# The last three pieces' products for the second tokens in two column halves, and the output in pieces of 1024 columns

## The chip, the cores and the metric

The kernel runs on one core of a Trainium2 chip. The metric is the device time of one execution in microseconds. A core has a matrix engine (TensorE; PE in the profile, with PEld for its weight loads), a vector engine (VectorE, DVE), an activation engine (ScalarE, ACT), GpSimd (POOL) and SyncE (SP), whose queue issues nearly all transfers here. Each engine works through its own queue in order; engines wait for each other through semaphores. Products are accumulated in PSUM, in banks of 512 fp32 columns on 128 partitions; everything else lies in SBUF.

## The reference

One layer of a gated short-convolution decoder, with 256 tokens of 2048 features, everything in fp32, and a normalization behind it:

```python
h = rmsnorm(x, norm_g[layer])
h, gate = adaln(h, c, ada_w[layer], ada_b[layer])
y = short_conv_mixer(h, sc_w_in[j], sc_conv_w[j], sc_w_out[j])
x = x + gate[:, None, :] * y
return rmsnorm(x, final_g)
```

`adaln` makes shift, scale and gate from a conditioning vector. The mixer projects 2048 features to four branches of 4096, convolves along the tokens over three taps, multiplies the branches together and projects 4096 back to 2048: `jnp.einsum('bse,ed->bsd', y, w_out)`. The last line needs, for every token, the mean of the squares of all 2048 features before any feature can be written.

## The kernel before

Weights and activations are each split into a high and a low part (`split` makes `hi` on ScalarE and `lo` on VectorE), and every product is the sum of three: high by high, high by low, low by high. The layer starts with the normalization and the conditioning, then come the input projection in pieces (line 430, tiles `mm_s` and `mm_b`, 256 tokens wide), the convolution and the gates, whose results `ys` stay in SBUF. Those parts are the same in both kernels.

The output projection runs over four column groups `dc` of 512 features. For each, the weights come in eight pieces (`ep`, four blocks of 128 rows each, 1 MB), and `out_mm` multiplies a piece by the tokens: 4 blocks x 3 products, each 128 tokens by 512 columns. The tokens are in two tiles of 128, the first (`t = 0`) and the second (`t = 1`). `po[0]` and `po[1]` are the accumulators of the two, each a PSUM bank of 512 columns.

The last group, `dc = 3`, differs. The gate is multiplied into the weights (line 668), and the banks are filled with the residual beforehand (line 656, ScalarE), so that what stands in a bank at the end is the new feature itself. `po[0]` and `po[1]` are in two different tiles of PSUM. For the last three pieces (`LATE = 3`) the second tokens' products are put off in the source: they stand behind the first tokens' end. So the first tokens are finished early: `gated(0, ...)` squares the bank on ScalarE and sums the squares into a column of `fsq` (line 685); `finish(0)` takes the root of that sum plus `part_sum`, the sum over the other three groups (line 633, which needs a change of ScalarE's table), its reciprocal on VectorE (line 634), multiplies the four column groups of the token tile by it (lines 639 to 643) and stores them (line 644). Then the 36 late products of the second tokens, `gated(1, ...)` and `finish(1)`.

The order in each queue isn't the source's alone. A scheduler with a cost model sets it when the program is built: some of the late products are pulled forward to places between the first tokens' products. The same layer puts in the semaphore waits: an instruction waits for those that wrote what it reads, and for those that read or wrote what it overwrites.

Of the kernel before, what the change touches and what calls it, by code (L numbers as in the profile page):

```python
# [10 lines left out]
AF = mybir.ActivationFunctionType  # L11
ALU = mybir.AluOpType

P = 128
D = 2048
# [113 lines left out]
def short_conv_layer(ctx: ExitStack, tc: tile.TileContext, x, c, norm_g, ada_w, ada_b, w_in, conv_w, w_out, final_g, out):  # L129
    nc = tc.nc  # L130
# [138 lines left out]
    for t in range(TT):  # L269
        for dh in range(2):  # L270
# [3 lines left out]
            else:  # L274
                nc.vector.scalar_tensor_tensor(
                    out=junk[:, t], in0=xt[t][dh], scalar=1.0, in1=xt[t][dh], op0=ALU.mult, op1=ALU.mult,
# [32 lines left out]
    scale = const.tile([P, KT], F32, tag="scale", name="scale")  # L309
# [21 lines left out]
    def split(raw, n, lo_tag="lo"):  # L331

        hi = wpool.tile([P, SLOT], F32R, tag="hi", name="hi", bufs=3)
        lo = wpool.tile([P, SLOT], F32R, tag=lo_tag, name="lo", bufs=3)
        nc.scalar.copy(hi[:, :n], raw[:, :n])  # L335
        nc.vector.tensor_tensor(out=lo[:, :n], in0=raw[:, :n], in1=hi[:, :n].bitcast(F32), op=ALU.subtract)  # L336
        return hi, lo
# [197 lines left out]
    def gate(dc):  # L535
        return gates[dc // 2][:, dc % 2, :]
# [31 lines left out]
    for ct in range(NS, NCT, 2):  # L568
        for q in QUARTERS:
            bank = psum.tile([P, CT, T], F32, tag="mm", name="mm_b")[:, 0:2]  # L570
            col = q * E + ct * P
            for kp in range(0, KT, KP):
# [5 lines left out]
                hi, lo = split(raw, SLOT)  # L578
                for m in range(2):
                    for i in range(KP):  # L580
                        k = kp + i
                        o = slice((i * 2 + m) * P, (i * 2 + m + 1) * P)
# [24 lines left out]
    big = hpool.tile([P, 4, D], F32, tag="big", name="big")  # L607
    fg = big[:, 2, :]
# [3 lines left out]
    fsq = const.tile([P, TT, 4], F32, tag="fsq", name="fsq")  # L612
    EP = 4
    LATE = 3

    def out_mm(po, t, ep, hi, lo):
        for i in range(EP):
            ct = ep * EP + i
            y = ys[ct // 2][:, ct % 2]
            yh = y[:, 0, t * P : (t + 1) * P]  # L620
            yl = y[:, 1, t * P : (t + 1) * P]
            o = slice(i * 512, (i + 1) * 512)
            opens = ct == 0 and dc < 3
            nc.tensor.matmul(po, yh, hi[:, o], start=opens, stop=False, skip_group_check=True)  # L624
            nc.tensor.matmul(po, yh, lo[:, o], start=False, stop=False, skip_group_check=True)  # L625
            nc.tensor.matmul(po, yl, hi[:, o], start=False, stop=ct == NCT - 1, skip_group_check=True)  # L626

    part_sum = const.tile([P, TT], F32, tag="part_sum", name="part_sum")

    def finish(t):  # L630

        fs = const.tile([P, 1], F32, tag="fs", name="fs", bufs=2)
        nc.scalar.activation(fs, fsq[:, t, 3:4], AF.Sqrt, bias=part_sum[:, t : t + 1])
        nc.vector.reciprocal(fs, fs)
        for c0, n, vector in ((0, 512, True), (512, 512, False), (1536, 512, True), (1024, 512, False)):
            dd = slice(c0, c0 + n)
            r = big[:, t, dd]
            if c0 == 1536:
                nc.vector.scalar_tensor_tensor(out=r, in0=po[t], scalar=fs, in1=fg[:, dd], op0=ALU.mult, op1=ALU.mult)
            elif vector:  # L640
                nc.vector.tensor_scalar_mul(r, r, fs)
            else:
                nc.scalar.activation(r, r, AF.Copy, scale=fs)  # L643
            nc.sync.dma_start(out[t * P : (t + 1) * P, dd], r)

    for dc in range(4):
        dcs = slice(dc * 512, (dc + 1) * 512)

        both = [psum.tile([P, TT, 512], F32, tag="mm", name="mm_o") for _ in range(1 + (dc == 3))]
        po = [both[-t][:, t] for t in range(TT)]  # L650
        n_ep = NCT // EP
        late = []
        if dc == 3:

            for t in range(TT):
                nc.scalar.copy(po[t], big[:, t, dcs])
        for ep in range(n_ep):

            first = dc == 0 and ep == 0
            raw = wpool.tile([P, SLOT], F32, tag="raw" if first else "lo", name="raw_o", bufs=3)  # L660
            nc.sync.dma_start(
                raw.rearrange("p (k f) -> p k f", k=EP),
                w_out[0, ep * EP * P : (ep + 1) * EP * P, dcs].rearrange("(k p) f -> p k f", p=P),
            )
            if dc == 3:

                raw3 = raw.rearrange("p (k f) -> p k f", k=EP)
                nc.vector.tensor_tensor(
                    out=raw3, in0=raw3, in1=gate(dc).unsqueeze(1).to_broadcast([P, EP, 512]), op=ALU.mult
                )  # L670
            hi, lo = split(raw, SLOT, "raw")
            out_mm(po[0], 0, ep, hi, lo)
            if dc == 3 and ep >= n_ep - LATE:
                late.append((ep, hi, lo))
            else:
                out_mm(po[1], 1, ep, hi, lo)

        def gated(t, bank, c0, n):

            cs = slice(dc * 512 + c0, dc * 512 + c0 + n)  # L680
            r = big[:, t, cs]
            p0 = (dc % 2) * 1024 + t * 512 + c0
            pr = big[:, 3, p0 : p0 + n]
            if dc == 3:
                nc.scalar.activation(pr, bank, AF.Square, scale=D**-0.5, accum_out=fsq[:, t, dc : dc + 1])
                return
            nc.vector.tensor_tensor(out=pr, in0=bank, in1=gate(dc)[:, c0 : c0 + n], op=ALU.mult)
            nc.vector.tensor_tensor(out=r, in0=r, in1=pr, op=ALU.add)
            nc.scalar.activation(pr, r, AF.Square, scale=D**-0.5, accum_out=fsq[:, t, dc : dc + 1])
            nc.vector.tensor_tensor(out=r, in0=r, in1=fg[:, cs], op=ALU.mult)  # L690
            if dc == 2:
                ps = part_sum[:, t : t + 1]
                nc.vector.reduce_sum(ps, fsq[:, t, 0:3], axis=mybir.AxisListType.X)
                nc.vector.tensor_scalar_add(ps, ps, EPS)

        gated(0, po[0], 0, 512)
        if dc == 3:
            finish(0)
        for ep, hi, lo in late:
            out_mm(po[1], 1, ep, hi, lo)  # L700
        gated(1, po[1], 0, 512)
    finish(1)


# [22 lines left out]
```

## Time and profile before

| what | us |
|---|---|
| median of 3 runs | 922.97 (922.72 to 924.28) |
| the profiled execution | 922.73 |
| its span, from first to last instruction | 921.0 |
| TensorE busy in it | 905.1 |
| granted TensorE clock, mean | 0.994 of full |

A profile row names the line of the code, the engine, the operation and the tiles. "Releaser" is what ended a wait. Starts are counted from the start of the span. The ends of products are modelled: in a dense row the time between two starts is the pace, and it is shorter than the duration shown. In the output stage all 768 products have the same shape, 128 tokens by 512 columns.

### The profile page before, as it was taken

What the parts mean: (1) busy time and instruction counts of PE and PEld (TensorE: products, weight loads), DVE (VectorE), ACT (ScalarE), POOL (GpSimd) and SP (SyncE); (2) the same over time, 40 slices, a digit from 0 to 9 for tenths busy, and PEclk for the clock granted to TensorE, in tenths of its full rate; (3) what the DMA queues carried; (4) which work ended last, traced back from release to release, by engine and by line L of the source; (5) the groups of instructions that cost most, each with busy time, mean ns of one, the idle gap of its engine ahead of it and who ended that gap; (6) DMA issues with size and microseconds to landing.
All of it is one profiled execution on the core that took longest, in us unless ns stands there. A gap on an engine that the chain in (4) does not pass through costs nothing.

```text
span 921.0 us, 16348 instructions
## 1 busy us (share of the span) xinstructions
PE 905.1 (98%) x7119; PEld 871.3 (95%) x7119; DVE 627.0 (68%) x601; ACT 450.3 (49%) x427; POOL 0.7 (0%) x6
## 2 busy tenths in 40 slices
PE   7899999999999999999999999999999999999996
PEld 7899999999999999999999999999999988888885
DVE  5888898999875899986545544555454535555882
ACT  3778975545544755544443334433444333443333
POOL 0000000000000000000000000000000000000000
PEclk9899999999999999999999999999999999999999
DMA  9999999999995569867566656665666486565542
GB/s 313 368 382 357 344 336 360 342 348 344 353 347 200 184 214 353 276 209 229 186 200 200 192 185 194 203 198 184 191 188 201 142 330 229 192 205 195 184 137 91
DMA packets 147367, 227.64 MB, mean 247 GB/s; under 512 B 5424, under 2 KB 103904, under 8 KB 146912
## 3 DMA queue, kind: packets, MB, share of 16 engines
q1 hardware_dynamic: 147056, 226.51, 73.2%
q8 instruction: 55, 0.90, 0.4%
q10 hardware_dynamic: 240, 0.09, 0.0%
q14 instruction: 16, 0.13, 0.0%
HBM read 224.49 MB, written 2.10 MB: 246 GB/s over the span
## 4 chain that ended last, share of the span: by engine, by line
PE 95%; DMA 3%; SPq 1%; DVE 0%; ACT 0%; ACTq 0%; issue 0%; DVEq 0%
PE mm_b L430 38%; PE mm_s L430 37%; PE mm_o L625 6%; PE mm_o L626 6%; PE mm_o L624 6%; DMA at<-in_ada_w_dram 2%; DMA x<-in_x_dram 1%; DMA raw_s<-in_sc_w_in_dram 1%; PE ps_gate L563 0%; SPq L223 0%; PE tp_g L419 0%; PE tp_x L305 0%; DVE lo L336 0%; SPq L203 0%; SPq L399 0%; ACT big L643 0%
## 5 line engine op out<-in xcount | busy, mean ns | idle before, releaser
L430 PE MATMUL mm_s<-hT,hi 128*128 128x256 f32 x2048 | 353.0, 278 | 1.0 <-ACT hT L325 0.5
L430 PE MATMUL mm_b<-hT,hi 128*128 128x256 f32 x2048 | 348.8, 276 | 0.0
L430 PEld LDWEIGHTS mm_s<-hT,hi 128*128 128x128 f32 x2048 | 310.6, 189 | 2.1 <-ACT hT L325 0.7
L430 PEld LDWEIGHTS mm_b<-hT,hi 128*128 128x128 f32 x2048 | 308.3, 188 | 0.2 <-issue 0.2
L430 PE MATMUL mm_s<-hT,lo 128*128 128x256 f32 x1024 | 283.1, 278 | 1.8 <-DVE lo L336 1.8
L430 PE MATMUL mm_b<-hT,lo 128*128 128x256 f32 x1024 | 282.6, 276 | 0.0
L336 DVE TENSOR_TENSOR lo<-raw,hi 128x2048 fp32r<-128x2048 f32 (+1 forms) x66 | 148.0, 2243 | 128.1 <-ACT hi L335 128.1
L335 ACT CAST hi<-raw 128x2048 fp32r<-128x2048 f32 (+1 forms) x66 | 123.7, 1874 | 203.8 <-PE mm_b L430 149.9
L430 PEld LDWEIGHTS mm_s<-hT,lo 128*128 128x128 f32 x1024 | 192.9, 189 | 2.0 <-DVE lo L336 2.0
L430 PEld LDWEIGHTS mm_b<-hT,lo 128*128 128x128 f32 x1024 | 192.2, 188 | 0.2 <-issue 0.2
L335 ACT CAST hi<-raw_s 128x2048 fp32r<-128x2048 f32 (+1 forms) x64 | 121.6, 1901 | 102.6 <-PE mm_s L430 88.9
L336 DVE TENSOR_TENSOR lo<-raw_s,hi 128x2048 fp32r<-128x2048 f32 (+1 forms) x64 | 145.4, 2273 | 33.2 <-ACT hi L335 30.3
L336 DVE TENSOR_TENSOR lo<-raw_o,hi 128x2048 fp32r<-128x2048 f32 x32 | 73.3, 2291 | 66.1 <-ACT hi L335 66.1
L335 ACT CAST hi<-raw_o 128x2048 fp32r<-128x2048 f32 x32 | 61.0, 1907 | 106.9 <-PE mm_o L626 88.0
L625 PE MATMUL mm_o<-lo,y 128*128 128x512 f32 x256 | 99.7, 391 | 0.0
L624 PE MATMUL mm_o<-hi,y 128*128 128x512 f32 x256 | 99.3, 389 | 0.0
L626 PE MATMUL mm_o<-hi,y 128*128 128x512 f32 x256 | 99.3, 389 | 0.0
L412 DVE SCALAR_TENSOR_TENSOR gv<-at,silu_c,gv 128x512 f32<-128x512 f32 x105 | 78.5, 749 | 2.5 <-DMA at<-in_ada_w_dram 0.8
L625 PEld LDWEIGHTS mm_o<-lo,y 128*128 128x128 f32 x256 | 48.1, 188 | 10.1 <-issue 0.2
L626 PEld LDWEIGHTS mm_o<-hi,y 128*128 128x128 f32 x256 | 48.0, 188 | 10.1 <-issue 0.2
L624 PEld LDWEIGHTS mm_o<-hi,y 128*128 128x128 f32 x256 | 48.1, 188 | 10.0
L451 ACT COPY acc<-mm_s 128x1024 f32<-128x1024 f32 x43 | 43.5, 1014 | 18.1 <-PE mm_s L430 18.0
(94 smaller groups left out, 382.2 us busy)
## 6 DMA issues: line engine op xcount, KB each, us to landing
raw<-in_sc_w_in_dram SPq DMA_DIRECT2D x64, 1024.0 KB, 5.6
raw_s<-in_sc_w_in_dram SPq DMA_DIRECT2D x63, 1024.0 KB, 7.0
raw_o<-in_sc_w_out_dram SPq DMA_DIRECT2D x32, 1024.0 KB, 5.2
at<-in_ada_w_dram SPq DMA_DIRECT2D x114, 256.0 KB, 6.8
at_g<-in_ada_w_dram SPq DMA_DIRECT2D x32, 512.0 KB, 7.0
at<-in_ada_w_dram SPq DMA_DIRECT2D x6, 512.0 KB, 8.8
x<-in_x_dram SPq DMA_DIRECT2D x4, 512.0 KB, 6.1
big<-in_x_dram SPq DMA_DIRECT2D x2, 1024.0 KB, 9.6
```

The lines of the kernel that those rows point to most:

```text
L335: nc.scalar.copy(hi[:, :n], raw[:, :n])
L336: nc.vector.tensor_tensor(out=lo[:, :n], in0=raw[:, :n], in1=hi[:, :n].bitcast(F32), op=ALU.subtract)
L412: nc.vector.scalar_tensor_tensor(out=gv, in0=at4[:, i], scalar=c_k, in1=gv, op0=ALU.mult, op1=ALU.add)
L430: mm = last_mm[0] = nc.tensor.matmul(dst, w, h[:, k], start=begins and left, stop=ends, skip_group_check=True)
L451: nc.scalar.copy(acc[ch, q], bank)
L624: nc.tensor.matmul(po, yh, hi[:, o], start=opens, stop=False, skip_group_check=True)
L625: nc.tensor.matmul(po, yh, lo[:, o], start=False, stop=False, skip_group_check=True)
L626: nc.tensor.matmul(po, yl, hi[:, o], start=False, stop=ct == NCT - 1, skip_group_check=True)
```

## The change

Two things change, both at the end of `dc = 3`.

The late products of the second tokens run over columns 0 to 255 of the bank first, all 36 of them, and then over columns 256 to 511, another 36; both halves are in the same PSUM bank. Each half is squared by itself. Both squares sum into the same column of `fsq`; VectorE adds the first one's sum to `part_sum` between the two.

`finish` works in two pieces of 1024 columns for both token tiles: ScalarE multiplies columns 512 to 1023 and VectorE 0 to 511, and one store of 512 KB writes both; then ScalarE takes 1024 to 1535, VectorE 1536 to 2047, and a second store writes these. Before, there were four stores of 256 KB.

```diff
-    def out_mm(po, t, ep, hi, lo):
+    def out_mm(po, t, ep, hi, lo, c0=0, n=512):
+        po = po[:, c0 : c0 + n]
...
-            o = slice(i * 512, (i + 1) * 512)
+            o = slice(i * 512 + c0, i * 512 + c0 + n)
...
-        for c0, n, vector in ((0, 512, True), (512, 512, False), (1536, 512, True), (1024, 512, False)):
-            dd = slice(c0, c0 + n)
-            r = big[:, t, dd]
-            if c0 == 1536:
-                nc.vector.scalar_tensor_tensor(out=r, in0=po[t], scalar=fs, in1=fg[:, dd], op0=ALU.mult, op1=ALU.mult)
-            elif vector:
-                nc.vector.tensor_scalar_mul(r, r, fs)
-            else:
-                nc.scalar.activation(r, r, AF.Copy, scale=fs)
-            nc.sync.dma_start(out[t * P : (t + 1) * P, dd], r)
+        r = big[:, t]
+        nc.scalar.activation(r[:, 512:1024], r[:, 512:1024], AF.Copy, scale=fs)
+        nc.vector.tensor_scalar_mul(r[:, 0:512], r[:, 0:512], fs)
+        nc.sync.dma_start(out[t * P : (t + 1) * P, 0:1024], r[:, 0:1024])
+        nc.scalar.activation(r[:, 1024:1536], r[:, 1024:1536], AF.Copy, scale=fs)
+        nc.vector.scalar_tensor_tensor(
+            out=r[:, 1536:D], in0=po[t], scalar=fs, in1=fg[:, 1536:D], op0=ALU.mult, op1=ALU.mult
+        )
+        nc.sync.dma_start(out[t * P : (t + 1) * P, 1024:D], r[:, 1024:D])
...
                 nc.scalar.activation(pr, bank, AF.Square, scale=D**-0.5, accum_out=fsq[:, t, dc : dc + 1])
+                if n < 512 and c0 == 0:
+                    ps = part_sum[:, t : t + 1]
+                    nc.vector.tensor_tensor(out=ps, in0=ps, in1=fsq[:, t, dc : dc + 1], op=ALU.add)
                 return
...
-        for ep, hi, lo in late:
-            out_mm(po[1], 1, ep, hi, lo)
-        gated(1, po[1], 0, 512)
+        for c0 in range(0, 512, 256 if late else 512):
+            for ep, hi, lo in late:
+                out_mm(po[1], 1, ep, hi, lo, c0, 256)
+            gated(1, po[1][:, c0 : c0 + (256 if late else 512)], c0, 256 if late else 512)
```

Line numbers of the changed kernel are shifted by up to four: `out_mm`'s three products are lines 625 to 627 there, the root 634, the reciprocal 635, the multiplies 637 to 641, the stores 639 and 644; the square stays 685.

TensorE's queue at its end, in the kernel before: the last products of the second tokens (`mm_o_9016` is the bank `po[1]`, `y14` and `y15` the activations of the last two pairs of blocks). No row of the late products waits there for anything.

```order
L624 MATMUL mm_o_9016<-hi_9215,y14_4514 128x512
L625 MATMUL mm_o_9016<-lo_9216,y14_4514 128x512
L626 MATMUL mm_o_9016<-hi_9215,y14_4514 128x512
L624 MATMUL mm_o_9016<-hi_9215,y15_4515 128x512
L625 MATMUL mm_o_9016<-lo_9216,y15_4515 128x512
L626 MATMUL mm_o_9016<-hi_9215,y15_4515 128x512
```

In the changed kernel, where the first half ends and the second begins (`hi_9177` and `y10` are the first of the late pieces):

```order
L625 MATMUL mm_o_9016<-hi_9215,y15_4515 128x256
L626 MATMUL mm_o_9016<-lo_9216,y15_4515 128x256
L627 MATMUL mm_o_9016<-hi_9215,y15_4515 128x256
L625 MATMUL mm_o_9016<-hi_9177,y10_4510 128x256 [waits Activation_49]
L626 MATMUL mm_o_9016<-lo_9178,y10_4510 128x256
L627 MATMUL mm_o_9016<-hi_9177,y10_4510 128x256
```

The 36 products have become 72, and the first of the second half waits for ScalarE; the count it waits for is that of the square of the first half. Of the late products, 14 stood ahead of the first tokens' last product before; now 15 of the first half's do.

ScalarE's queue, from the square of the first tokens (`mm_o_9015`) to the end, before:

```order
L685 ACTIVATE big_8258,fsq_8262<-mm_o_9015 128x512 [waits PE_49]
L633 ACT_TABLE_LOAD
L633 ACTIVATE fs_9232<-fsq_8262,part_sum_8263 128x1 [waits Activation_49]
L643 ACTIVATE big_8258<-big_8258,fs_9232 128x512 [waits DVE_49]
L643 ACTIVATE big_8258<-big_8258,fs_9232 128x512
L685 ACTIVATE big_8258,fsq_8262<-mm_o_9016 128x512 [waits PE_49]
L633 ACTIVATE fs_9280<-fsq_8262,part_sum_8263 128x1 [waits Activation_49]
```

And now:

```order
L685 ACTIVATE big_8258,fsq_8262<-mm_o_9015 128x512 [waits PE_49]
L634 ACT_TABLE_LOAD
L634 ACTIVATE fs_9232<-fsq_8262,part_sum_8263 128x1 [waits Activation_49]
L637 ACTIVATE big_8258<-big_8258,fs_9232 128x512 [waits DVE_49]
L640 ACTIVATE big_8258<-big_8258,fs_9232 128x512
L685 ACTIVATE big_8258,fsq_8262<-mm_o_9016 128x256 [waits PE_49]
L685 ACTIVATE big_8258,fsq_8262<-mm_o_9016 128x256 [waits DVE_49,PE_49]
L634 ACTIVATE fs_9316<-fsq_8262,part_sum_8263 128x1 [waits Activation_49]
```

One square has become two, both behind the five steps of the first tokens; the second of them also waits for VectorE's addition.

## The prediction

> **What bounds the kernel now.** I read the page first: the shares of the engines, then the chain that ended last.
>
> ```profile
> span 921.0 us, 16348 instructions
> PE 905.1 (98%) x7119; PEld 871.3 (95%) x7119; DVE 627.0 (68%) x601; ACT 450.3 (49%) x427; POOL 0.7 (0%) x6
> PE 95%; DMA 3%; SPq 1%; DVE 0%; ACT 0%; ACTq 0%; issue 0%; DVEq 0%
> ```
>
> TensorE carries 95% of the chain, so anything that makes it stand still is paid in full, and anything that follows its last product is paid too. The profiled execution took 922.73 us, 1.73 more than its span; the median of the runs is 922.97. The change touches only the end, so next I read the timeline from 908 us on (start, duration, engine, line).
>
> ```profile
> 908.03 0.61 PE L626 MATMUL mm_o<-hi,y 128*128 128x512 f32 x2
> 908.46 0.60 ACT L685 ACTIVATE big<-mm_o 128x512 f32<-128x512 f32 x1 [9.39 <-PE mm_o L626]
> 908.49 0.39 PE L624 MATMUL mm_o<-hi,y 128*128 128x512 f32 x1
> ...
> 909.17 1.28 ACT L633 ACT_TABLE_LOAD   x1
> ...
> 910.99 1.34 ACT L643 ACTIVATE big<-big,fs 128x512 f32<-128x512 f32 x2 [0.23 <-DVE fs L634]
> ...
> 912.57 0.39 PE L624 MATMUL mm_o<-hi,y 128*128 128x512 f32 x1
> ...
> 913.02 0.39 PE L626 MATMUL mm_o<-hi,y 128*128 128x512 f32 x1
> 913.44 0.60 ACT L685 ACTIVATE big<-mm_o 128x512 f32<-128x512 f32 x1 [1.12 <-PE mm_o L626]
> ...
> 914.16 0.29 ACT L633 ACTIVATE fs<-fsq,part_sum 128x1 f32<-128x1 f32 x1
> 914.49 0.16 DVE L634 RECIPROCAL fs<-fs 128x1 f32<-128x1 f32 x1 [2.36 <-ACT fs L633]
> 914.69 1.34 ACT L643 ACTIVATE big<-big,fs 128x512 f32<-128x512 f32 x2 [0.23 <-DVE fs L634]
> 914.69 0.49 DVE L641 TENSOR_SCALAR big<-big,fs 128x512 f32<-128x512 f32 x1
> ```
>
> The first tokens' last product starts at 908.03 (the first of the two in that row) and ends at 908.42; ScalarE then runs their square, table load, root and two multiplies until 910.99 + 1.34 = 912.33, while TensorE goes on with the second tokens until 913.02 + 0.39 = 913.41. So ScalarE is free 1.12 us before it is needed again. Then the square, the root, the reciprocal and the multiplies of the second tokens stand bare, and last the stores:
>
> ```profile
> 915.21 0.81 SPq L644 DMA_DIRECT2D out_dram<-big  x2
> ...
> 916.60 0.41 SPq L644 DMA_DIRECT2D out_dram<-big  x1
> DMA to landing us min/median/max: 2.3/2.9/3.2
> SPq L723 <- DMA out_dram<-big: 2.8, 1, 2.8
> GB/s 255 255 108 54 0 0 0 161 403 403 416 417 417 403 376 309 430 349 309 336 363 403 363 282 282 215 175 54 13 0 0 0 0 0 0 0 0 0 0 0
> ```
>
> The four stores of the second tokens are issued from 915.21 to 916.60; the first to be issued lands 2.3 us later, the last 3.2 us later, at 919.8, and 1.2 us of closing follow. The last line is what all DMA engines moved from 914.9 to 921 us, in slices of 0.15 us: from about 916.1 to 918.4 they run near 400 GB/s.
>
> **The change, part by part.**
>
> *Pace of halved products.* These rows of the earlier stage, in which every product has 256 columns, give the price (count, durations in ns, first and last start):
>
> ```profile
> L430 PE MATMUL mm_b<-hT,hi x2048: 276/276/680, 389.2 to 738.0; 128*128 128x256 f32 x187
> L430 PE MATMUL mm_b<-hT,lo x1024: 276/276/281, 389.4 to 738.1; 128*128 128x256 f32 x171
> ```
>
> 3072 starts from 389.2 to 738.1 are 0.1136 us each. With 512 columns, 908.49 to 912.57 holds 18 steps: 0.2267 us. So 72 halves cost 8.18 against 8.16 for 36 wholes: +0.02 us in all, although each half loads its weights again.
>
> *First tokens end earlier.* By the rows of both programs, 14 whole products of the second tokens stand ahead of the first tokens' last product before, and 15 halves now: 14 x 0.2267 - 15 x 0.1136 = 1.47 us. The square of the first tokens starts at 908.46 - 1.47 = 906.99, and ScalarE's five steps (3.87 us, 908.46 to 912.33) last until 910.86.
>
> *The new wait, the main term.* In the changed program the first product of the second half waits for ScalarE (the row with the wait is shown with the change above), although no product of that half writes a column that the first square reads. The semaphore's count in that wait is that of the first half's square. That square stands in ScalarE's queue behind the first tokens' five steps. Step by step: the first tokens' last product starts at 908.03 - 1.47 = 906.56; the 21 halves left start from 906.79 to 909.06, and the last ends (0.28) at 909.34. ScalarE could square only at 910.86. A square of 256 columns has no row; 512 columns took 598 ns and a like read of PSUM with 128 columns 262 ns (below), so 374 ns by the straight line, 0.22 less. From a square's start to the next step were 0.72 us (913.44 to 914.16); half of it takes 0.50, done at 911.34 or so.
>
> ```profile
> L685 ACT ACTIVATE big<-mm_o 128x512 f32<-128x512 f32 x2 | 1.2, 598 | 10.5 <-PE mm_o L626 10.5
> L421 ACT ACTIVATE tp_g<-tp_g 128x128 f32<-128x128 f32 x28 | 7.3, 262 | 0.5
> ```
>
> TensorE starts again 0.06 us after its releaser (see the rows from 37 us below: 34.89 + 2.28 = 37.17 to 37.23), at 911.40. It stands still for 2.06 us. Everything on TensorE is queued behind that product: 36 halves, 35 x 0.1136 + 0.28, and about 0.1 for a first weight load that nothing covers: the end is 915.75, 2.34 us later than 913.41.
>
> *Shorter last square.* 0.22 us gained: the closing multiplies start at 914.69 + 2.34 - 0.22 = 916.81. Squaring in two costs one more square (already counted) and one addition of a column on VectorE, about 0.16 us like the reciprocal of one column, which runs while TensorE does the second half: nothing. If the second half were to start at once, that addition would still have 4 us of cover.
>
> *Stores.* Four issues become two; the first waits for ScalarE's first multiply, the second for its second. They are issued at 916.81 + 0.72 + 0.03 = 917.56 (before, at +0.52, behind VectorE's shorter multiply) and 916.81 + 1.34 + 0.03 = 918.18. The lower bound of the last landing is that of a store that meets an idle queue: 2.3 us for 256 KB plus 0.65 for 256 KB more at 405 GB/s, 918.18 + 2.95 = 921.13. The upper one is that the same megabyte flows as it did, 915.21 to 919.8 or 4.59 us from the first issue: 922.15. The engines were nearly full in most of that stretch, so I stay near the upper end: 922.0. The first tokens' two stores go out at about 910.4 and 911.0 and are long gone.
>
> *Sum.* 922.0 + 1.2 = 923.2 against 921.0: +2.2 us (bounds +1.3 to +2.35), 924.9 us.
>
> *What a standstill of 2 us costs besides.* The only like standstill of the trace is at the start. TensorE's rows there, VectorE's row that ended the gap, and then TensorE by stretches of a microsecond (busy time, products, granted clock, DMA share, GB/s; the last row, from the end, has the other engines between):
>
> ```profile
> 33.67 0.28 PE L430 MATMUL mm_s<-hT,lo 128*128 128x256 f32 x1
> 34.07 0.50 PE L430 MATMUL mm_s<-hT,hi 128*128 128x256 f32 x2
> 34.97 0.50 PE L430 MATMUL mm_s<-hT,hi 128*128 128x256 f32 x2 [0.40 <-ACT acc L451]
> 37.23 0.58 PE L430 MATMUL mm_s<-hT,lo 128*128 128x256 f32 x1 [1.76 <-DVE lo L336]
> ...
> 38.04 0.41 PE L430 MATMUL mm_s<-hT,lo 128*128 128x256 f32 x1
> ...
> 38.68 0.41 PE L430 MATMUL mm_s<-hT,lo 128*128 128x256 f32 x1
> 34.89 2.28 DVE L336 TENSOR_TENSOR lo<-raw_s,hi 128x2048 fp32r<-128x2048 f32 x1
> 36.00:37.00 1.00, 0.00 (x0) 0.96 1.04 414
> 37.00:38.00 1.00, 0.77 (x3) 0.50 1.01 384
> 39.00:40.00 1.00, 1.00 (x7) 0.50 1.07 348
> 40.00:41.00 1.00, 1.00 (x9) 0.83 1.09 347
> 917.00:918.00 1.00, 0.00 (x0) 0.00 (x0) 0.00 (x0) 0.00 (x0) 0.00 (x0) 0.78 1.08 356
> ```
>
> A gap of 1.76 us let the clock fall to 0.50 at 36.92 (a mean of 0.96 in that microsecond); it came back at 40.34, 3.42 us later, and 917.56 at the end lies on the same grid of 3.41 us (258 steps from 36.92). So the clock is decided at the ticks of a grid from what the last 3.41 us held: 1.97 us idle (0.12 + 0.40 + 1.45) made it fall, and 0.74 us idle, from 913.41 to the tick at 914.15, did not. While it is down, seven products fit in a microsecond instead of nine to ten, or 0.213 us between starts in place of 0.1136 (38.04 to 38.68 are three products): 3.41 x (1 - 0.1136/0.213) = 1.6 us lost. The new standstill of 2.06 us lies wholly between two ticks in (3.41 - 2.06)/3.41 = 40% of phases, and then the clock falls; with a limit of 1.35 us idle, midway between the two rows, in about 80%. I see nothing that ties the grid to the start of the program, so I take somewhat over half, and add 1.6 us to the likeliest case: 924.9 + 1.6 = 926.5.
>
> The Trainium skill, "TensorE: Matmul & The Clock Gate", section "The HAM clock gate", lets the clock fall only after one whole idle window of about 3.4 us; by it nothing falls here, and the sum stays at 924.9. This trace speaks against it: 1.97 us of idle time in one such stretch sufficed.
>
> **The rivals.**
> *Standstill, but the clock stays up*: 924.9 us (924.1 to 925.2 by the bounds of the stores). For it: with the grid of this execution the tick at 910.73 would split the standstill into 1.39 and 0.67 us, both under 1.97. Against it: the phases above.
> *No standstill, not slower*: it decides at ScalarE being free by 908.9, so that the half square is done when TensorE reaches 909.4. Then only the 0.02, the 0.22, and the stores (+0.24 to -0.8) are left: 922.73 - 0.3, or 922.4. Against it: ScalarE's five steps last 3.87 us, of which 1.28 are the table load, and TensorE has 2.4 us of work to cover them. Even the best end of the stores, 921.7, would be within what a measurement of this kernel tells from no change, 0.2% or 1.85 us.
> *Clock down for the whole second half*: 36 x (0.213 - 0.1136) = 3.6 instead of 1.6: 928.5. Against it: at 40.34 one stretch of busy products raised it.
>
> **How the numbers follow.** Standstill with the clock falling 0.52, 926.5 us; standstill alone 0.38, 924.9; no standstill 0.06, 922.4; clock down throughout 0.04, 928.5. The point is the likeliest, 926.5 (its own range 925.6 to 926.8). Runs of both phases may mix, so the range takes in both standstill cases: 924.0 to 927.0. Slower by over 0.2% means above 924.82 (922.97 x 1.002): the first case, the last, and a little over half of the second, 0.78; within 0.2%: 0.20; faster by over 0.2%: 0.02.
>
> **What would show it.** After: TensorE's waits with one on ScalarE's square (L685) of about 2 us near 909 us; the first square of the second tokens directly behind the two multiplies (L637, L640); products of 256 columns 0.114 us apart, and 0.21 apart in a stretch of up to 3.4 us with a granted clock of 0.50; the last square near 0.37 us; two stores of 512 KB issued 0.6 us apart. The forecast is wrong if TensorE goes on at 909.4 without a wait, if the clock reads 1.00 until the end, or if the stores of 4 KB rows flow at another rate than those of 2 KB.

## The result

The changed kernel takes 926.05 us (median of 16 runs, 922.33 to 927.73) against 923.29 us for the kernel before (16 runs, 920.96 to 924.28). The ratio is 1.0028, with a 95% interval of 1.0019 to 1.0038: slower by about 0.28%. The forecast was 926.5 us, within 924.0 to 927.0.

The profiled execution of the changed kernel took 926.89 us. Its page and TensorE's longest wait in the output stage (engine, line, releaser: us in all, times, longest):

```profile
span 925.1 us, 16416 instructions
PE mm_o L625 <- ACT big L685: 1.8, 1, 1.8
```

The wait that the forecast rests on is there, once, for ScalarE's square. The timeline of ScalarE at the end (start, duration, engine, line):

```profile
908.19 0.60 ACT L685 ACTIVATE big<-mm_o 128x512 f32<-128x512 f32 x1 [8.09 <-PE mm_o L627]
...
908.90 1.28 ACT L634 ACT_TABLE_LOAD   x1
...
911.35 0.71 ACT L640 ACTIVATE big<-big,fs 128x512 f32<-128x512 f32 x1
911.96 0.36 ACT L685 ACTIVATE big<-mm_o 128x256 f32<-128x256 f32 x1
...
918.58 0.38 ACT L685 ACTIVATE big<-mm_o 128x256 f32<-128x256 f32 x1 [6.16 <-PE mm_o L627]
...
919.61 0.72 ACT L637 ACTIVATE big<-big,fs 128x512 f32<-128x512 f32 x1 [0.23 <-DVE fs L635]
```

The first half's square starts at 911.96, directly behind the five steps of the first tokens. The two stores of the second tokens go out 0.74 and 1.36 us after the closing multiplies at 919.61:

```profile
920.35 0.33 SPq L639 DMA_DIRECT2D out_dram<-big  x1
920.97 0.33 SPq L644 DMA_DIRECT2D out_dram<-big  x1
```

TensorE in the same stretch, and below it TensorE by microseconds (busy time, products, granted clock, DMA share, GB/s):

```profile
910.38 0.28 PE L627 MATMUL mm_o<-hi,y 128*128 128x256 f32 x1
912.47 0.39 PE L625 MATMUL mm_o<-hi,y 128*128 128x256 f32 x1 [1.80 <-ACT big L685]
...
918.26 0.28 PE L627 MATMUL mm_o<-hi,y 128*128 128x256 f32 x1
```

```profile
912.00:913.00 1.00, 0.53 (x4) 1.00 0.71 291
913.00:914.00 1.00, 1.00 (x8) 0.59 1.02 418
...
915.00:916.00 1.00, 1.00 (x7) 0.50 0.00 0
916.00:917.00 1.00, 1.00 (x8) 0.70 0.00 0
917.00:918.00 1.00, 1.00 (x10) 1.00 0.00 0
```

TensorE stands still from 910.66 to 912.47, and 0.7 us after it has started again the granted clock falls to one half. A mean of 0.59 in the microsecond from 913 puts the fall at 913.18; 0.70 in that from 916 puts the rise at 916.60, 3.42 us later.

**A common measure for all runs.** The span of one execution also holds the start of the program, where the clock falls at other places each time. In both kernels ScalarE's last split of weights is the same step just ahead of the change:

```profile
897.17 1.90 ACT L335 CAST hi<-raw_o 128x2048 fp32r<-128x2048 f32 x1 [3.53 <-PE mm_o L626]
```

```profile
898.20 1.90 ACT L335 CAST hi<-raw_o 128x2048 fp32r<-128x2048 f32 x1 [3.53 <-PE mm_o L627]
```

The first is of the kernel before, the second of the changed one. So 1.03 us of the 4.1 us between the two spans lie ahead of the change and are none of its doing. From here on, "the end" of a kernel is the time from the start of its last split to the end of its span: 921.0 - 897.17 = 23.83 us before, 925.1 - 898.20 = 26.90 after, so the change costs 3.07 us in this execution. Spans are given to 0.1 us, so differences between ends of less than 0.1 us mean nothing.

### The profile page after: what moved, and what is told of

It is laid out like the page before. It is cut to its first block, busy times and chain, and to the rows that moved or that the text cites. A ratio compares the mean times of both kernels' runs of the same rounds, so it can differ in the third digit from the quotient of the medians.

```text
span 925.1 us, 16416 instructions
## 1 busy us (share of the span) xinstructions
PE 906.7 (98%) x7155; PEld 873.6 (94%) x7155; DVE 627.4 (68%) x602; ACT 450.5 (49%) x429; POOL 0.7 (0%) x6
## 4 chain that ended last, share of the span: by engine, by line
PE 95%; DMA 2%; SPq 1%; ACT 1%; DVE 0%; issue 0%; ACTq 0%; DVEq 0%
PE mm_b L430 38%; PE mm_s L430 37%; PE mm_o L625 6%; PE mm_o L627 6%; PE mm_o L626 6%; DMA raw<-in_sc_w_in_dram 1%; DMA at<-in_ada_w_dram 1%; DMA x<-in_x_dram 1%; SPq L223 1%; SPq L399 0%; PE ps_gate L563 0%; PE tp_g L419 0%; PE tp_x L305 0%; DVE lo L336 0%; ACT big L685 0%; ACT big L637 0%
## 5 line engine op out<-in xcount | busy, mean ns | idle before, releaser
L625 PE MATMUL mm_o<-hi,y 128*128 128x512 f32 (+1 forms) x268 | 102.2, 383 | 1.8 <-ACT big L685 1.8
L626 PE MATMUL mm_o<-lo,y 128*128 128x512 f32 (+1 forms) x268 | 102.6, 384 | 0.0
L627 PE MATMUL mm_o<-hi,y 128*128 128x512 f32 (+1 forms) x268 | 102.3, 382 | 0.0
L625 PEld LDWEIGHTS mm_o<-hi,y 128*128 128x128 f32 x268 | 51.1, 191 | 11.5 <-ACT big L685 2.0
L626 PEld LDWEIGHTS mm_o<-lo,y 128*128 128x128 f32 x268 | 51.0, 191 | 9.8 <-issue 0.2
L627 PEld LDWEIGHTS mm_o<-hi,y 128*128 128x128 f32 x268 | 51.1, 191 | 9.7 <-issue 0.2
```

## The experiments

Nine kernels were run, one of them twice. The end comes from the profile of each, the ratio from its timed runs beside runs of the kernel before on the same chip.

| kernel | median us | ratio to before, 95% interval | span | end |
|---|---|---|---|---|
| before | 923.29 | | 921.0 | 23.83 |
| changed | 926.05 | 1.0028 (1.0019 to 1.0038) | 925.1 | 26.90 |
| larger stores alone | 921.12 | 0.9986 (0.9974 to 0.9999) | 920.1 | 22.95 |
| larger stores alone, again | 922.89 | 0.9993 (0.9981 to 1.0005) | 921.1 | 23.00 |
| halves alone | 924.39 | 1.0025 (1.0010 to 1.0039) | 921.6 | 26.13 |
| halved products, one square | 923.82 | 1.0011 (1.0001 to 1.0020) | 922.5 | 24.26 |
| gap filled, first try | 924.22 | 1.0021 (1.0009 to 1.0032) | 924.4 | 26.68 |
| gap filled | 924.55 | 1.0018 (1.0008 to 1.0027) | 923.0 | 25.41 |
| second half in its own tile | 922.84 | 0.9998 (0.9986 to 1.0010) | 919.6 | 23.28 |
| first half's square moved ahead | 924.04 | 1.0014 (1.0004 to 1.0024) | 922.6 | 24.19 |
| four stores with long rows | 924.74 | 1.0024 (1.0012 to 1.0036) | 922.6 | 25.31 |
| four stores with short rows | 922.64 | 1.0004 (0.9992 to 1.0015) | 920.9 | 23.82 |

### Each part alone

*The larger stores alone.* The kernel before, with the new `finish` and nothing else:

```diff
-        for c0, n, vector in ((0, 512, True), (512, 512, False), (1536, 512, True), (1024, 512, False)):
...
-            nc.sync.dma_start(out[t * P : (t + 1) * P, dd], r)
+        nc.sync.dma_start(out[t * P : (t + 1) * P, 0:1024], r[:, 0:1024])
...
+        nc.sync.dma_start(out[t * P : (t + 1) * P, 1024:D], r[:, 1024:D])
```

> The kernel before with the output change alone: two stores of 1024 columns for each token tile, the products whole. The end is measured from the start of the last weight split on ScalarE (line 335) to the end of the span, 23.83 us before and 26.90 us after, so that the start of the program, where the clock falls at other places in each run, is left out. If the two stores are a gain of their own, 0.8 us as the rows of after suggest (5.49 us from the closing multiplies to the end against 6.31), the end takes 23.0 us and the ratio to before is about 0.999. If the two larger stores only look shorter there because they start later, the end stays at 23.8 and the ratio at 1.000. If they cost part of the loss, it is above 24.

The end is 22.95 us, 0.88 shorter, and 23.00 (0.83 shorter) when it was run again:

> The two larger stores alone once more, as the version that should beat both kernels: end 22.95 us as in the first run of it, and a ratio to before of 0.9985 to 0.9995 (0.9 us of 923).

The two ratios are 0.9986 and 0.9993; the second interval includes 1. The two issues of the second tokens, and what all DMA engines moved from 914.9 to 921 us in slices of 0.15 us, the same stretch as in the prediction:

```profile
914.67 0.72 ACT L636 ACTIVATE big<-big,fs 128x512 f32<-128x512 f32 x1 [0.23 <-DVE fs L634]
...
915.42 0.33 SPq L638 DMA_DIRECT2D out_dram<-big  x1
916.03 0.33 SPq L643 DMA_DIRECT2D out_dram<-big  x1
```

```profile
GB/s 430 27 0 0 0 0 0 0 134 430 430 322 430 430 403 430 403 430 430 430 430 430 403 430 430 54 0 0 0 0 0 0 0 0 0 0 0 0 0 0
```

The multiplies start where they did before (914.69), and the first store goes out 0.2 us later than the first of four did. But the rate stands near 430 GB/s up to the last bytes, where the four stores fell off through 282, 215 and 175, and the last store, issued 0.57 us earlier (916.03 against 916.60), lands after the same 3.2 us. In both profiles the larger stores gain some 0.85 us; the timed runs fit that, but only one of the two intervals excludes no change.

*The halves alone.* The changed kernel with the old `finish` of four stores.

> The products in halves alone, with the four stores of 512 columns as before. If the halves carry the whole loss and the stores gain 0.8 us, the end takes 27.7 us with the clock falling in the second half and about 26.1 without, and the ratio to before is about 1.0035. If the stores carry the loss, the end takes 23.6 us and the ratio is 1.000 or below.

The end is 26.13 us, 2.30 longer than before. TensorE's stop has the length that it has in the changed kernel, 1.80 us, but the clock stays up while TensorE works:

```profile
907.66 0.28 PE L627 MATMUL mm_o<-hi,y 128*128 128x256 f32 x1
909.75 0.39 PE L625 MATMUL mm_o<-hi,y 128*128 128x256 f32 x1 [1.80 <-ACT big L686]
909.97 0.28 PE L626 MATMUL mm_o<-lo,y 128*128 128x256 f32 x1
```

```profile
910.00:911.00 1.00, 1.00 (x10) 1.00 1.08 375
...
914.00:915.00 1.00, 0.32 (x3) 1.00 0.00 0
...
919.00:920.00 1.00, 0.00 (x0) 0.62 0.59 197
```

It falls after the last product, at 919.24. On a grid of 3.413 us three ticks before that is 909.00, which lies within the stop (907.94 to 909.75) and splits it into 1.06 and 0.75 us.

*Halved products, one square.* The halves alone, but squared once, over all 512 columns, when both are done:

```diff
         for c0 in range(0, 512, 256 if late else 512):
             for ep, hi, lo in late:
                 out_mm(po[1], 1, ep, hi, lo, c0, 256)
-            gated(1, po[1][:, c0 : c0 + (256 if late else 512)], c0, 256 if late else 512)
+        gated(1, po[1], 0, 512)
```

> The kernel before with the 36 late products as 72 halves, but one square over the whole bank at the end as before, and the four stores as before: no wait between the halves. If a half costs 0.120 us as in the profiles of the changed kernels, and not the 0.1136 of the input projection, TensorE has no gap, and the end takes 24.3 us, 0.5 more than before. If the slower pace comes from the wait or the clock, the halves go at 0.1136 and the end stays at 23.85.

TensorE doesn't stop, and the end is 24.26 us: the 72 halves alone cost 0.43 us. At the start of the last square it is 0.55 us (915.06 - 898.24 = 16.82 after the last split, against 913.44 - 897.17 = 16.27); what follows the square took about 0.1 us less in this execution. The last product and the one six before it, and the square behind them:

```profile
914.02 0.28 PE L627 MATMUL mm_o<-hi,y 128*128 128x256 f32 x1
...
914.75 0.28 PE L627 MATMUL mm_o<-hi,y 128*128 128x256 f32 x1
915.06 0.60 ACT L686 ACTIVATE big<-mm_o 128x512 f32<-128x512 f32 x1 [2.96 <-PE mm_o L627]
```

Six steps in 0.73 us are 0.12 us each, where the input projection's products of the same shape were 0.1136 apart.

### What makes TensorE stop, and what the stop costs

*The first half's square moved ahead.* If ScalarE's queue is the cause, the stop should shrink to the square itself once the square doesn't stand behind `finish(0)`:

```diff
...
-        if dc == 3:
-            finish(0)
...
+            if late and c0 == 0:
+                with behind({squared[-1].engine: squared[-1].name}):
+                    finish(0)
```

> The changed kernel with ScalarE's queue in another order: the first half's square stands ahead of the first tokens' table load, root and multiplies instead of behind them. If the length of the wait is the first half's square's place in ScalarE's queue, TensorE's gap falls from 1.80 us to 0.55 (the square and its sum 0.5, and the restart), too short for the clock to fall, and the end takes 24.0 us, about 0.2 more than before; ratio 1.000. If the wait is for something else, the gap stays at 1.8 us and the end at 25.3 or 26.9.

```profile
910.60 0.28 PE L627 MATMUL mm_o<-hi,y 128*128 128x256 f32 x1
911.44 0.39 PE L625 MATMUL mm_o<-hi,y 128*128 128x256 f32 x1 [0.56 <-ACT big L686]
```

```profile
910.92 0.39 ACT L686 ACTIVATE big<-mm_o 128x256 f32<-128x256 f32 x1 [1.82 <-PE mm_o L627]
...
911.41 1.28 ACT L635 ACT_TABLE_LOAD   x1
```

Now the table load follows the half square, and 0.56 us of the stop are left: the square's 0.39 us and the ways to and from it. The end is 24.19 us with the larger stores in it, 2.71 shorter than the changed kernel's. The place in ScalarE's queue thus makes 1.24 of the 1.80 us, and 0.56 remain for as long as the second half waits for the square at all.

*The second half in its own tile.* In the changed kernel both halves lie in one tile and in one bank. Here the second half gets another tile of PSUM, in another bank; nothing is left out. All second-token products of `dc = 3` are then halves, and VectorE's closing multiply goes in two:

```diff
-        po = po[:, c0 : c0 + n]
+        po = halves[c0 // 256] if n < 512 else po
...
+            halves = [po[1][:, 0:256], psum.tile([P, 512], F32, tag="sm", name="mm_h", bufs=2)[:, 0:256]]
```

> The changed kernel with the second half in a PSUM tile of its own, in another bank, so that nothing in it depends on the first half's square; all products of the second tokens in the last column group are halves here, and VectorE's closing multiply of the accumulator goes in two pieces. If the wait for that square is the cause, TensorE has no gap at the end, the clock stays at 1.00, and the end takes 23.0 to 23.4 us, less than the kernel before by the shorter square and the stores; the ratio to before is 0.999 to 1.0005, since 60 more products of 256 columns come in ahead. If the gap comes from ScalarE being late for another reason, or the halves themselves are slow, the gap or the slow pace stays and the end is above 25 us.

```profile
909.94 0.36 ACT L690 ACTIVATE big<-mm_o 128x256 f32<-128x256 f32 x1
...
913.11 0.39 ACT L690 ACTIVATE big<-mm_h 128x256 f32<-128x256 f32 x1 [2.73 <-PE mm_h L627]
```

```profile
909.92 0.28 PE L627 MATMUL mm_h<-hi,y 128*128 128x256 f32 x1
...
910.28 0.28 PE L627 MATMUL mm_h<-hi,y 128*128 128x256 f32 x1
```

The first square comes behind the first tokens' steps as ever, and nobody waits for it: TensorE works on `mm_h` right through it. The end is 23.28 us, 3.62 shorter than the changed kernel's, and the ratio to the kernel before is 0.9998. The sums don't need the wait, since no product of the second half writes a column that the first square reads. But tile and bank were changed together here, so this run doesn't say which of the two the wait belongs to, and whether ScalarE may read one half of a bank while TensorE writes the other was not tried.

*The gap filled.* To price the clock by itself, products whose result nobody reads were put where TensorE stands still. The wait stays; only the idle time goes. In the first try they went into the tile of the first tokens' bank:

```diff
+            if late and c0 == 0:
+                for _ in range(15):
+                    nc.tensor.matmul(both[0][:, 1, 0:256], ys[0][:, 0, 0, 0:P], late[0][1][:, 0:256], start=True, stop=True, skip_group_check=True)
```

> The changed kernel with 15 more products of 256 columns into a bank that nobody reads, between the two halves: TensorE has some 1.8 us of work while it would stand still, the wait of the second half stays. If the clock falls because TensorE stands still, it reads 1.00 throughout here, the halves keep 0.12 us to the end, and the end takes 25.3 us (1.6 less than after) whatever the phase; the time falls towards 924.6 us, ratio about 1.0013, and no run loses the 1.6 us. If the slow stretch belongs to the halves or to their weight loads, the slow products stay and the end takes 26.9 us or more.

That was a miss of the experiment, with a use of its own. The filler waited in turn for VectorE's last read of that tile, ran too late and held up the second half until 913.34. It wrote the tile's second bank (`both[0][:, 1]`) and VectorE read the first (`both[0][:, 0]`), so here the wait covered both banks of the tile:

```profile
909.91 0.28 PE L627 MATMUL mm_o<-hi,y 128*128 128x256 f32 x1
911.45 2.06 PE L708 MATMUL mm_o<-hi,y 128*128 128x256 f32 x15 [1.26 <-DVE big L641]
913.34 0.28 PE L625 MATMUL mm_o<-hi,y 128*128 128x256 f32 x1
```

```profile
914.00:915.00 1.00, 1.00 (x10) 1.00 0.35 139
...
922.00:923.00 1.00, 0.00 (x0) 0.75 0.98 401
```

The clock falls at 922.50, so there is a tick of the grid at 908.85 and one at 912.26, and the idle 1.26 us (910.19 to 911.45) lie wholly between them. That was not enough to make it fall. In the second try the filler had a bank of its own and one product less:

```diff
+                idle_bank = psum.tile([P, 512], F32, tag="sm", name="idle_bank", bufs=2)
+                for _ in range(14):
+                    nc.tensor.matmul(idle_bank[:, 0:256], ys[0][:, 0, 0, 0:P], late[2][1][:, 0:256], start=True, stop=True, skip_group_check=True)
```

> The changed kernel with 14 products of 256 columns, 1.7 us of work, between the two halves, this time into a bank that no other work of the end uses, so that they start as soon as the first half ends; the wait of the second half stays. If standing still is what lets the clock fall, TensorE's gap is 0.2 us or less, the clock reads 1.00 to the end in every phase, and the end (from the last weight split on ScalarE to the end of the span) takes 25.3 us as against 26.9 in the profile of after, 2.3 (halves) - 0.9 (stores) over before; the ratio to before is about 1.0015. If the clock falls for another reason, slow products 0.21 us apart appear again in profiles and the time stays near 926 us.

```profile
909.89 1.84 PE L709 MATMUL idle_bank<-hi,y 128*128 128x256 f32 x14
911.86 0.39 PE L625 MATMUL mm_o<-hi,y 128*128 128x256 f32 x1
```

```profile
913.00:915.00 2.00, 2.00 (x19) 1.00 0.61 250
```

The second half starts 14.27 us after the last split (911.86 - 897.59), exactly as in the changed kernel (912.47 - 898.20), so TensorE's useful work is held up just as long. But the clock reads 1.00, and the end is 25.41 instead of 26.90 us: the fall of the clock costs 1.49 us. The halves alone, whose clock stayed up, give 26.90 - (26.13 - 0.85) = 1.62. The timed runs can't settle it, because a run's mean clock takes in the falls at the start of the program too: 0.992 or less was granted in eleven of the changed kernel's 16 runs and in one of this one's 11, but also in five of 11 of the larger stores alone when run again, which have no such stop.

### Why the larger stores are faster

The larger stores have longer rows (4 KB instead of 2 KB), are half as many, and go out at other times. Two kernels keep the new `finish` and cut each of its stores in two:

```diff
-        nc.sync.dma_start(out[t * P : (t + 1) * P, 0:1024], r[:, 0:1024])
+        for p in (0, 64):
+            nc.sync.dma_start(out[t * P + p : t * P + p + 64, 0:1024], r[p : p + 64, 0:1024])
```

> The larger stores alone, but each 1024-column store is issued as two of 64 partitions: four stores of 256 KB again, with rows of 4 KB. From the start of the last weight split to the end of the span it took 23.83 us before and 22.95 and 23.00 with two stores of 512 KB. If the gain comes from the longer rows, it stays: 23.0. If it comes from having two issues in place of four, it goes: 23.8. If only the later time of the last issue counts (0.35 us later, behind one more issue), 23.35.

```diff
-        nc.sync.dma_start(out[t * P : (t + 1) * P, 0:1024], r[:, 0:1024])
+        for c in (0, 512):
+            nc.sync.dma_start(out[t * P : (t + 1) * P, c : c + 512], r[:, c : c + 512])
```

> The larger stores alone, but each 1024-column store is issued as two of 512 columns one behind the other: four stores of 256 KB with rows of 2 KB, at the times of the kernel with the larger stores. If the gain comes from the longer rows, it goes: 23.8, and the rate falls off before the last byte as in the kernel before. If it comes from two issues in place of four, it goes too: 23.8. If only the time of the last issue counts, 23.35.

The issues of the second tokens in the two kernels, and for the second one what the DMA engines moved from 914.9 to 921 us:

```profile
915.56 1.11 SPq L639 DMA_DIRECT2D out_dram<-big  x2
916.77 1.71 SPq L645 DMA_DIRECT2D out_dram<-big  x2
```

```profile
915.12 0.81 SPq L639 DMA_DIRECT2D out_dram<-big  x2
916.02 0.91 SPq L645 DMA_DIRECT2D out_dram<-big  x2
```

```profile
GB/s 242 202 94 14 0 0 67 349 389 403 403 417 403 416 349 403 376 282 255 309 390 376 390 322 282 175 107 14 0 0 0 0 0 0 0 0 0 0 0 0
```

With short rows the whole gain is gone (23.82 against 23.83), and the rate falls off at the end as in the kernel before. But, other than its expectation says, this kernel didn't keep the times of the larger stores. Counted from the closing multiplies (914.60 here), its first store goes out at 0.52 and its last at 1.92 us, as in the kernel before (0.52 and 1.91); with two larger stores it is 0.75 and 1.36. So it is nearly the kernel before once more, and the time of the last issue isn't ruled out as a cause.

With long rows on 64 partitions the end is not 23.0 but 25.31, which none of the expectations had: each such store takes 0.5 to 1.0 us in SyncE's queue instead of 0.33 to 0.36, and lands after 3.1 to 4.1 us instead of 2.6 to 3.3. Halving the partitions thus brought a cost of its own, and this run says nothing about long rows alone.

What the traces do show is where the gain lies. Over all 128 partitions the last store lands 3.2 us after its issue, whether it is the last of four or of two. With two it is issued 0.55 us sooner, and from its landing to the end of the span it is about 0.9 us (920.1 - 919.23) instead of 1.2 (921.0 - 919.8); together that is the 0.85 us. Whether longer rows or fewer stores make this possible stays open.

## Why the prediction came out

The point (926.5 against 926.05) and the sign were right, and the mechanism was the one forecast. Of its terms two were clearly mis-sized, in opposite directions. All are us of the end of the profiled execution:

| term | forecast | measured | from |
|---|---|---|---|
| pace of the halves | +0.02 | +0.43 | halved products, one square: 24.26 - 23.83 |
| TensorE's stop and restart | +2.32 | +2.07 | halves alone: 907.66 to 909.75 less one step of 0.12, and the step after it 0.22 instead of 0.12 |
| shorter last square | -0.22 | -0.22 | 0.38 against 0.60 |
| stores and closing | +0.08 | -0.85 | larger stores alone, twice: -0.88, -0.83 |
| fall of the clock | +1.6 | +1.49 | gap filled: 26.90 - 25.41 |
| sum | +3.8 | +2.92 | the end: 3.07 |

The measured terms leave 0.15 us of the 3.07 unaccounted for; with the pace as 0.55, measured at the start of the last square, they reach 3.04. The first three give 2.28 against the 2.30 of the halves alone.

*Pace of halved products: wrong.* The step took 0.1136 us from the input projection for products of the same shape. In the output projection they are 0.120 apart. 72 x 0.0064 is 0.46 us. A price from another stage was taken for this one.

*First tokens end earlier: right, a little less.* The first tokens' square starts 11.29 us after the last split before (908.46 - 897.17) and 9.99 after (908.19 - 898.20): 1.30 instead of 1.47, because the halves among the last products ahead are slower than thought.

*The new wait: right in place, cause and queue.* Forecast were 2.06 us, measured 1.80. ScalarE was as late as forecast, but TensorE got there about 0.3 us later, by the pace. The kernel with the square moved ahead shows that the queue makes 1.24 us of it, the one with a tile of its own that nothing else stops TensorE there. Whether the wait is there for the tile or for the bank stays open.

*Shorter last square: right*, 0.36 and 0.38 us for the two halves against 0.374; and the added column on VectorE cost nothing that shows.

*Stores: wrong.* The step had bounds of 921.13 and 922.15 for the last landing and took 922.0, "the engines were nearly full in most of that stretch". From the start of the closing multiplies to the end of the span it forecast 6.39 us (916.81 to 923.2); the changed kernel took 925.1 - 919.61 = 5.49, the kernel before 921.0 - 914.69 = 6.31. The issues came as forecast (0.74 and 1.36 us after the multiplies, against 0.75 and 1.37). Mis-sized were the flight of the last store, 3.2 us instead of 922.0 - 918.18 = 3.82, and the closing, about 0.9 us instead of 1.2. The lower bound, 921.13 + 1.2 - 916.81 = 5.52, comes close to 5.49 only because its landing was some 0.25 us too early and its closing 0.3 too long. The row of GB/s in the prediction held a hint: its last six slices with bytes in them, from 282 down to 13, are not those of a full engine. One of the prediction's own signs of being wrong came true with this: the stores of 4 KB rows did flow at another rate than those of 2 KB, near 430 GB/s up to the last bytes.

*The clock: it fell as forecast, but half of the rule behind it doesn't hold.* The fall lasted 3.42 us, as at the start, and cost 1.49 against 1.6: 16 halves in it were 0.213 us apart in place of 0.120. Whether it falls hangs on the phase, as forecast: the same 1.80 us make it fall where they lie between two ticks (909.77 to 913.18 here) and don't where a tick splits them (the halves alone). So the ticks of the grid held. The limit of idle time, put between 0.74 and 1.97 us, did not. The changed kernel's own trace has two stretches from tick to tick in which TensorE was idle for nearly the same time, 1.45 and 1.48 us. The clock falls after the first and stays up after the second (busy time, products, granted clock, DMA share, GB/s):

```profile
32.54:35.96 3.42, 1.97 (x13) 1.00 1.04 410
35.96:39.37 3.41, 2.25 (x10) 0.50 1.04 375
...
916.60:920.01 3.41, 1.94 (x16) 1.00 0.00 0
920.01:923.43 3.42, 0.00 (x0) 1.00 0.68 278
```

The trace that the prediction read has such a case as well, which it left out: from 23.27 to 26.69 us TensorE was busy for 2.73 of 3.42 us, though with products of 1 and 128 columns, and the clock fell at 26.69. So idle time by the profile's rows isn't all that decides; what else does stays open. The chances that rested on the limit of 1.35 us have no support, and that the clock fell in the profiled execution was partly luck.

The Trainium skill, "TensorE: Matmul & The Clock Gate", section "The HAM clock gate", asks for a whole idle window of about 3.4 us, by which the changed kernel's clock would not have fallen; here it fell after 1.80 us.

*The rivals.* "Standstill, but the clock stays up" is what the halves alone did in their profile, and what some runs of the changed kernel may do: its range of 5.4 us would hold both, but no profile of such a run was kept. "No standstill, not slower" is the kernel with its own tile. "Clock down for the whole second half" didn't occur.

So the likeliest case was right for its reason, but its point came closer than its sum. The forecast added 3.8 us to the 922.73 of the profiled execution; the ends differ by 3.07 us and the medians of 16 runs by 2.76, with the errors of pace (+0.4), standstill (-0.25) and stores (-0.9) partly cancelling. That the point is off by only 0.45 us is also luck: the median of the kernel before is 0.56 us above the 922.73 that it started from.

Of all kernels run, the larger stores alone have the shortest end, 0.85 us shorter than before, and ratios 0.07 to 0.14% below one, of which one interval includes no change. The halves gained nothing in the forms tried: even without the wait, and with the larger stores in it, the end of 23.28 us is longer than those 22.95 to 23.00. By the timed runs the two can't be told apart, since their intervals overlap.

## What to carry to other kernels

Cutting a step in two so that its first half is finished early made the second half wait for whoever reads the first, as long as both halves lay in one tile and bank; ask where that reader stands in its own queue, since here five unrelated steps ahead of it made 1.24 of 1.80 us. A stop of TensorE costs its own length, and where it let the clock fall it cost nearly as much again (1.80 and 1.49 us here). The price of a step is to be taken from the stage in which it will run. And for the last stores it pays to follow the last one alone, from its issue to its landing: here two stores brought its issue forward by 0.55 us.

## What the runs showed of the hardware

- Products of 256 columns were 0.1136 us apart in the input projection and 0.120 in the output projection, at the same granted clock of 1.00 and with the same shapes. What differs was not settled.
- Stores over 64 of the 128 partitions, with the same bytes and rows of 4 KB, took 0.5 to 1.0 us each in SyncE's queue against 0.33 to 0.36 us for a store of twice the bytes over all partitions, and the end was 1.48 us longer than with four stores of 2 KB rows.
- The granted clock changed at ticks 3.413 us apart. 1.80 us idle between two ticks made it fall for one whole stretch (909.77 to 913.18 in the changed kernel), and 1.80 us cut by a tick did not (the halves alone). But 1.45 us made it fall at 35.96 and 1.48 us did not at 920.01, both in the changed kernel, so the idle time of a stretch doesn't decide it alone.
